# The last norm of a two-layer decoder trunk: its scales spread without a diagonal, one root for both sums, and one scaling moved behind the last sum

## The chip, the cores and the metric

The kernel runs on one core of a Trainium2 chip. The metric is the device time of one execution in microseconds (us). A core has a matrix engine (PE, with its weight loads listed apart as PEld), a vector engine (DVE), a scalar engine (ACT), GpSimd (POOL) and a queue engine (SP). Matrix products land in PSUM, which has eight banks of 512 f32 columns; POOL has no access to PSUM in this kernel. SP and ACT issue the transfers.

## What is computed

The reference runs two sub-layers over 1056 tokens (1024 of a prompt, 32 of a sample batch) of width 1024. The part that matters here is the end: the output projection of the second layer, the residual sum, and the final RMS norm.

```python
def _rmsnorm(x, gain):
    xf = x.astype(jnp.float32)
    y = xf * lax.rsqrt(jnp.mean(xf * xf, axis=-1, keepdims=True) + EPS)
    return (y * gain.astype(jnp.float32)).astype(x.dtype)

# _hgrn_layer ends with
    y = (o.reshape(Bsz, T, INNER_B) * jax.nn.silu(gate)).astype(x.dtype)
    return x + y @ w_out, S_T.astype(x.dtype)

# _trunk ends with
    return _rmsnorm(x, final_gain), jnp.stack(hs), jnp.stack(bufs), jnp.stack(Ss)
```

For each token, the squares of its 1024 values are summed, the root of their mean is inverted, and each value is multiplied by that scale and by its column's gain.

## The kernel before, in words

Activations are kept transposed: 8 tiles x2[k] of 128 features (partitions) by 1056 tokens (columns). In the profile these tiles carry the names of the buffers that they live in: k = 0 is ST, 1 to 3 are R, 4 is a, 5 to 7 are sg. A sum over features is thus a sum over partitions, which PE makes with a product with ones.

The last stage is the loop `for a, n in OUT` (L1762 on). It takes the tokens in three spans of n = 512, 288 and 256 columns. For each span it goes through the 8 tiles m = 0 to 7:

- PE makes the last three eighths of the output projection, 9 products of n columns (lines 262 to 264), into one of three banks.
- DVE adds that bank to x2[m] (L1781).
- ACT squares x2[m] (L1783).
- POOL adds the square to an accumulator `acc` (L1792). In the last span the squares of m = 4 to 7 aren't added by POOL; PE sums them straight into the column sums, behind all the products of the span.

The norm of a span is finished while the next span is worked on. At m = RM = 3 of the next span, `summed` has PE sum `acc` over partitions (`norm_sum`, L299), which puts the sum of token j of a group of 128 on partition j, one group to a column. `roots` then takes a root for each group on ACT (L1724), one reciprocal on DVE (L1727), and makes a diagonal on DVE (L1728, and L1732 for a rest of under 128): the identity times the reciprocal. At m = SM = 6, `spread` has PE multiply a matrix of ones by that diagonal (L1738), which puts the scale of token j on all partitions of column j of one bank. `finish` scales the 8 tiles with that bank and the gain. For the span of 512 all eight are done on DVE straight from PSUM (L1758). For the later spans tiles 5 to 7 go another way: ACT copies the bank to SBUF (L1751) and multiplies the tile by the gain (L1755), POOL multiplies by the copied scale (L1756). Each finished tile is written out by a transfer (L332), tiles of even k from SP, of odd k from ACT.

After the last span, PE runs two products of ones with ones (`spin`, L1796), and then the same roots, diagonal, spread and finish follow for the last 256 columns, now with nothing else running.

All of this is recorded into a `Flow` object, which plans the order of instructions on every engine from estimated costs (`add`, `plan`, `back`, `search`). Operations marked main=True on PE (the products, the `summed` sums and the spreads inside the loop) keep the order in which they are written. An engine carries out its instructions in the planned order, and waits at the first one that isn't ready. A transfer issued by ACT stands in ACT's own order, and ACT waits there until its tile is finished.

Two readers of one PSUM bank are kept apart: the second waits for a semaphore of the first.

Of the kernel before, what the change touches and what calls it, by code (L numbers as in the profile page):

```python
# [18 lines left out]
AF = mybir.ActivationFunctionType  # L19
ALU = mybir.AluOpType  # L20
# [11 lines left out]
SPOTS, SPOTS0, SPOTS1 = (-1, -1, 0, 2), (2, 5, -1, -1), (1, 5, 9, 13, 17, 20)  # L32
K2 = 8 - K1
NB4 = 6
RM, SM = 3, 6
OUT = ((0, 512), (512, 288), (800, 256))

D = 1024
# [192 lines left out]
def tile_trunk(ctx: ExitStack, tc: tile.TileContext, xT, prm, hc, w0, wg, wo0, w1, wo1, s_in,  # L231
# [18 lines left out]
    def pc(name, j, n=1):  # L250
        a = PRM[name][0] + j
        return P[:, a:a + n]
# [40 lines left out]
    def spans(n):  # L293
        return [(a, min(128, n - a)) for a in range(0, n, 128)]

    def norm_sum(sums, acc, n, start, stop):

        for s, (a, u) in zip(sums, spans(n)):
            T.matmul(s[:u], acc[:, a:a + u], ones[:, :1], start=start, stop=stop)  # L299

    def new_acts():
        hs, ls = [], []
# [15 lines left out]
    with ExitStack() as l0:  # L318
# [15 lines left out]
        def act(n, emit, r, w, prio=5, more=0.0):  # L334
            fl.add("ACT", 0.08 + 0.00086 * n + more, emit, r, w, prio)
# [5 lines left out]
        def pool(n, emit, r, w, prio=5):  # L341
            fl.add("POOL", 0.15 + 0.0022 * n, emit, r, w, prio)
# [609 lines left out]
    with ExitStack() as l1:  # L952
# [782 lines left out]
        def spread(n, dg, dk, main):  # L1735
# [2 lines left out]
            fl.add("PE", 0.002 * n, lambda: T.matmul(bc[:, :n], ones, dg, start=True, stop=True), (dk,), (bk,), 0, main=main)  # L1738
            return bc[:, :n], bk

        def summed(acc, ak, n):
            s, sk = next(hg)
            sums = [s[:, i:i + 1] for i in range(4)]
            fl.add("PE", 0.7, lambda: norm_sum(sums, acc, n, True, True), (ak,), (sk,), 0, main=True)
            return roots(n, sums, (sk,))

        def finish(a, n, bc, bk):
            q = slice(a, a + n)
            own = KD - 3 if a else KD
            if a:  # L1750
                act(n, lambda: S.copy(sb[0][:, :n], bc), (bk,), (sb[1],), 0)  # L1751
            for k in (*range(own, KD), *range(own)):
                x, xk = x2[k][:, q], ykeys(Y2 + k, a, n)
                if k >= own:
                    act(n, lambda x=x, k=k: S.activation(x, x, AF.Copy, scale=pc("gf", k)), xk, xk, 1)  # L1755
                    pool(n, lambda x=x: G.tensor_tensor(x, x, sb[0][:, :n], op=ALU.mult), (sb[1], *xk), xk, 1)  # L1756
                else:
                    dve(n, lambda x=x, k=k: V.scalar_tensor_tensor(x, x, pc("gf", k), bc, op0=ALU.mult, op1=ALU.mult), (bk, *xk), xk, 1)  # L1758
                dma(yT[k][:, q], x, xk, (), 1, n / 2, S if k % 2 else Q)

        for a, n in OUT:
            q = slice(a, a + n)  # L1762
            final = a + n == TOK
            cs = [c for c in range(NCH) if c * CH < a + n and (c + 1) * CH > a]
            acc, ak = next(accs)
            for m in range(KD):
                if a and m == RM:
                    dg = summed(*prev[:2], prev[3])
                if a and m == SM:
                    finish(*prev[2:], *spread(prev[3], *dg, True))  # L1770
                ps, pk = next(mm)
                hi, lo, wk = late[m]

                def emit(ps=ps, hi=hi, lo=lo, q=q, n=n):
                    for k in range(K2):
                        w = slice(128 * k, 128 * k + 128)
                        mm3(ps[:, :n], (hi[:, w], lo[:, w]), yh[K1 + k][:, q], yl[K1 + k][:, q], k == 0, k == K2 - 1)

                pe(9 * n / 2200, emit, (*wk, *((o, K1 + k, c) for o in ("xh", "xl") for k in range(K2) for c in cs)), (pk,))
                x, xk = x2[m][:, q], ykeys(Y2 + m, a, n)  # L1780
                dve(n, lambda x=x, ps=ps, n=n: V.tensor_tensor(x, ps[:, :n], x, op=ALU.add), (pk, *xk), xk, 0)  # L1781
                sq, sk = next(sqs) if m else (acc, ak)
                act(n, lambda sq=sq, x=x, n=n: S.activation(sq[:, :n], x, AF.Square), xk, (sk,), 1)  # L1783
                if final and m >= 4:
                    if m == 4:
                        sums = [(next(hg)) for _ in spans(n)]
                        sumk = [k for _, k in sums]
                        sums = [s[:, :1] for s, _ in sums]
                        fl.add("PE", 0.3, lambda acc=acc, n=n, sums=sums: norm_sum(sums, acc, n, True, False), (ak,), sumk, 0)
                    fl.add("PE", 0.3, lambda sq=sq, n=n, m=m, sums=sums: norm_sum(sums, sq, n, False, m == KD - 1), (sk, *sumk), sumk, 0)  # L1790
                elif m:
                    pool(n, lambda acc=acc, sq=sq, n=n: G.tensor_tensor(acc[:, :n], acc[:, :n], sq[:, :n], op=ALU.add), (sk, ak), (ak,), 1)  # L1792
            prev = acc, ak, a, n
        spin, wk = next(mm)
        for _ in range(2):
            fl.add("PE", 0.45, lambda: T.matmul(spin[:, :128], ones, ones, start=True, stop=True), sumk, (wk,), 0)  # L1796
        finish(a, n, *spread(n, *roots(n, sums, sumk), False))
        with tc.manual_schedule(engines={E.PE, E.DVE, E.Activation, E.Pool, E.SP}):
            fl.run(SEARCH, 60.0)

# [69 lines left out]
```

## Time and profile before

| | |
|---|---|
| median of 3 runs | 1032.07 us (1031.61 to 1032.12) |
| profiled execution | 1031.86 us |
| its span, first to last instruction | 1030.1 us, at a mean granted clock of 0.997 |
| PE busy | 1021.1 us (99%) |
| DVE, ACT, POOL busy | 810.8, 578.1, 496.5 us |
| last product of the output projection starts | 1019.11 us |
| last sum on PE starts | 1021.33 us |
| first scaling of the last span starts | 1024.08 us |
| last transfer is issued | 1026.43 us |

A row of the timeline reads: start (us from the span's start), duration (us), engine, line, operation, output <- inputs, shapes and types, number of merged instructions; in brackets the idle time of the engine before it and what ended it. A row of the windows table gives the stretch, its length, the busy time of PE, PEld, DVE, ACT and POOL with numbers of instructions, the granted PE clock, the share of the DMA engines and GB/s. On f32 operands each product written in the kernel shows as two weight loads and two matmuls.

### The profile page before, as it was taken

The page shows a single profiled execution, that of the slowest core. Times are in us where ns is not written, and L with a number is a line of the kernel's source. Part 1 is how long each engine was busy: PE and PEld are TensorE (multiplying, and loading weights), DVE is VectorE, ACT ScalarE, POOL GpSimd, SP SyncE. Part 2 cuts the span into 40 slices and gives each one's busy share as a digit, 9 for nine tenths or more (in the row PEclk, how much of TensorE's full clock was granted, in tenths as well). Part 3 has the DMA queues.
Part 4 walks back from the last instruction along what each step waited for, and adds up shares of the span by engine and source line. Part 5 has one row for each costly group of instructions (what it writes and reads, how often), then busy time and mean ns, then how long its engine had stood idle before and what let it go on. Part 6 is the DMA issues. An engine that isn't in the chain of part 4 may idle for free.

```text
span 1030.1 us, 26451 instructions
## 1 busy us (share of the span) xinstructions
PE 1021.1 (99%) x10118; PEld 996.4 (97%) x10118; DVE 810.8 (79%) x1641; ACT 578.1 (56%) x1322; POOL 496.5 (48%) x569
## 2 busy tenths in 40 slices
PE   9999999999999999999999999999999999999997
PEld 9999999999999999999999999999999999999986
DVE  7999785867888699436599999798989799986436
ACT  8788747876775785335454463626363636552334
POOL 0117353544526236636425656555555557533544
PEclk9999999999999999999999999999999999999998
DMA  9201112112852487426474244343535353687204
GB/s 299 78 17 56 57 48 74 52 54 76 257 178 59 133 270 223 160 83 219 136 213 138 73 147 132 130 148 111 167 111 168 102 159 122 207 246 209 87 1 169
DMA packets 107854, 138.30 MB, mean 134 GB/s; under 512 B 23632, under 2 KB 85072, under 8 KB 107728
## 3 DMA queue, kind: packets, MB, share of 16 engines
q1 hardware_dynamic: 105424, 133.85, 42.1%
q10 hardware_dynamic: 2304, 2.77, 0.8%
q8 instruction: 79, 1.29, 0.5%
q14 instruction: 47, 0.39, 0.1%
HBM read 89.99 MB, written 41.61 MB: 128 GB/s over the span
## 4 chain that ended last, share of the span: by engine, by line
PE 93%; DVE 2%; DMA 2%; ACT 1%; issue 1%; POOL 1%; SPq 0%; POOLq 0%; DVEq 0%; ACTq 0%
PE mm L262 27%; PE mm L264 26%; PE mm L263 26%; PE hg L1085 2%; PE hg L592 1%; PE hg L262 1%; PE hg L264 1%; PE hg L263 1%; PE hg L753 1%; PE hg L1232 1%; PE hg L1287 1%; PE hg L1289 1%; DMA k<-yd 1%; PE mm L1085 0%; DMA vt<-sg 0%
## 5 line engine op out<-in xcount | busy, mean ns | idle before, releaser
L262 PE MATMUL mm<-xh,whi 128*128 128x352 f32 (+1 forms) x1127 | 352.6, 313 | 0.1
L264 PE MATMUL mm<-xh,wlo 128*128 128x352 f32 (+1 forms) x1127 | 348.1, 309 | 0.0
L263 PE MATMUL mm<-xl,whi 128*128 128x352 f32 (+1 forms) x1127 | 347.7, 309 | 0.0
L346 POOL TENSOR_TENSOR wlo<-wraw,whi 128x256 fp32r<-128x256 f32 (+3 forms) x188 | 200.8, 1084 | 199.7 <-ACT whi L403 97.3
L263 PEld LDWEIGHTS mm<-xl,whi 128*128 128x128 f32 x1127 | 212.5, 189 | 1.4 <-DVE xl L346 0.3
L262 PEld LDWEIGHTS mm<-xh,whi 128*128 128x128 f32 x1127 | 211.8, 188 | 2.1 <-DVE k L1545 0.3
L264 PEld LDWEIGHTS mm<-xh,wlo 128*128 128x128 f32 x1127 | 212.0, 188 | 0.0
L524 DVE SCALAR_TENSOR_TENSOR k<-xb,prm_sb,k 128x352 f32<-128x352 f32 (+2 forms) x144 | 82.3, 596 | 24.2 <-ACT k L521 20.7
L262 PE MATMUL mm<-t,whi 128*128 128x264 f32 (+1 forms) x330 | 96.6, 293 | 0.2 <-issue 0.2
L264 PE MATMUL mm<-t,wlo 128*128 128x264 f32 (+1 forms) x330 | 94.4, 286 | 0.0
L263 PE MATMUL mm<-t,whi 128*128 128x264 f32 (+1 forms) x330 | 94.4, 286 | 0.0
L1545 DVE TENSOR_TENSOR k<-mm,k 128x264 f32<-128x264 f32 x154 | 64.0, 424 | 11.7 <-PE mm L264 10.3
L346 POOL TENSOR_TENSOR wlo<-R,whi 128x256 fp32r<-128x256 f32 x70 | 58.3, 854 | 27.0 <-ACT whi L1469 24.1
L607 POOL TENSOR_TENSOR k<-X 128x352 f32<-128x352 f32 x36 | 43.6, 1217 | 52.8 <-DVE R L608 42.0
L1469 ACT CAST whi<-wraw 128x512 fp32r<-128x512 f32 x56 | 34.5, 618 | 60.4 <-DVE wraw L1479 26.0
L403 ACT CAST whi<-wraw 128x512 fp32r<-128x512 f32 (+2 forms) x79 | 44.3, 572 | 39.1 <-PE mm L263 28.9
L262 PEld LDWEIGHTS mm<-t,whi 128*128 128x128 f32 x330 | 62.1, 188 | 1.5 <-issue 0.3
L263 PEld LDWEIGHTS mm<-t,whi 128*128 128x128 f32 x330 | 62.2, 188 | 0.0
L264 PEld LDWEIGHTS mm<-t,wlo 128*128 128x128 f32 x330 | 62.1, 188 | 0.0
L262 PE MATMUL mm<-yh,whi 128*128 128x352 f32 x153 | 52.2, 341 | 0.0
L264 PE MATMUL mm<-yh,wlo 128*128 128x352 f32 x153 | 49.4, 323 | 0.0
L263 PE MATMUL mm<-yl,whi 128*128 128x352 f32 x153 | 49.4, 323 | 0.0
(458 smaller groups left out, 2513.9 us busy)
## 6 DMA issues: line engine op xcount, KB each, us to landing
wraw<-in_w_dram SPq DMA_DIRECT2D x88, 256.0 KB, 3.0
wraw<-in_wo_dram SPq DMA_DIRECT2D x34, 192.0 KB, 2.5
R<-in_w_dram SPq DMA_DIRECT2D x17, 256.0 KB, 3.9
si<-in_s_in_dram SPq DMA_DIRECT2D x8, 512.0 KB, 5.4
vt<-sg SPq DMA_DIRECT2D x8, 512.0 KB, 3.8
sg<-vt SPq DMA_DIRECT2D x32, 128.0 KB, 2.9
kt<-kt SPq DMA_DIRECT2D x8, 512.0 KB, 3.6
kt<-kt SPq DMA_DIRECT2D x32, 128.0 KB, 5.1
```

What stands on the lines that cost most here:

```text
L262: T.matmul(out, wh, xh, start=first, stop=False)
L263: T.matmul(out, wh, xl, start=False, stop=False)
L264: T.matmul(out, wl, xh, start=False, stop=last)
L346: emit = lambda: e.tensor_tensor(b, x, a.bitcast(F32), op=ALU.subtract)
L403: act(m, lambda hi=hi, raw=raw, m=m: S.copy(hi[:, :m], raw[:, :m]), rk, (hk,), prio)
L524: dve(u, lambda src=src, dst=dst, sh=sh, k=k: V.scalar_tensor_tensor(dst, sh(src, k), pc("cw", 12 * k + m), dst, op0=ALU.mult, op1=ALU.add ...
L592: fl.add("PE", 0.62, lambda ps=ps, i=i, c=c: T.matmul(ps[:96, :CH], gs[:, i, :], ST[:96, chunk(c)], start=True, stop=True), (("gs",), *((" ...
L607: pool(CH, lambda x=x, a=a, b=b: G.tensor_tensor(x, a.bitcast(F32), b.bitcast(F32), op=ALU.add), (ak, bk), (xk,), 3)
L753: fl.add("PE", 0.25, lambda: T.matmul(warm[:, :128], ones, ones, start=True, stop=True), (), (wk,), 9)
L1085: T.matmul(ps[32 * j:32 * j + 32, n * w:n * w + w], B[:, o:o + 32], q(slice(o, o + 32)), start=True, stop=True, tile_position=(0, 32 * j))
L1469: act(512, lambda: S.copy(hi, raw), (rk,), (hk,), 2)
L1545: dve(QT, lambda: V.tensor_tensor(o[0], z[0], u[0], op=ALU.add), (z[1], u[1]), (o[1],), 0)
```

## The change

Four edits, all in the last stage.

- The spread of the **last** span no longer takes a diagonal. `spread_last` takes the column of reciprocals r of a group of 128 as the stationary operand, repeated over 128 columns with a step of zero, and the identity as the moving one; the product holds r[j] in column j on all partitions. It is called twice, into two banks: ACT copies the first, DVE scales from the second.
- `last_sum` puts both sums of the last span into two columns of one bank, so that one root (L1822 of the new file) takes both; only the first product clears the bank.
- SM goes from 6 to 5: the spread of the preceding span stands ahead of tile 5 of the running span, and not ahead of tile 6. This holds for the span of 512 (finished within the span of 288) and for the span of 288 (finished within the span of 256).
- When the span of 288 is finished, tiles 4 to 7 go by ACT and POOL (before: 5 to 7), tiles 0 to 2 are scaled on DVE at once, and tile 3 is scaled on DVE only after the last sum of x2[7] (L1805 of the new file), by `rest`.

```diff
-RM, SM = 3, 6
+RM, SM = 3, 5
...
+    def last_sum(s, acc, n, first, last):
+
+        for i, (a, u) in enumerate(spans(n)):
+            T.matmul(s[:u, i:i + 1], acc[:, a:a + u], ones[:, :1], start=first and not i, stop=last, skip_group_check=True)
...
+        def spread_last(n, r, rk):
+
+            bc, bk = next(hg)
+
+            def emit():
+                for i, (a, u) in enumerate(spans(n)):
+                    T.matmul(bc[:, a:a + u], r[:, i:i + 1].to_broadcast([128, 128]), ident, start=True, stop=True)
+
+            fl.add("PE", 0.0018 * n, emit, (rk,), (bk,), 0)
+            return bc[:, :n], bk
...
-        def finish(a, n, bc, bk):
+        def scaled(k, q, a, n, bc, bk, after=()):
+
+            x, xk = x2[k][:, q], ykeys(Y2 + k, a, n)
+            dve(n, lambda: V.scalar_tensor_tensor(x, x, pc("gf", k), bc, op0=ALU.mult, op1=ALU.mult), (bk, *xk, *after), xk, 1)
+            dma(yT[k][:, q], x, xk, (), 1, n / 2, S if k % 2 else Q)
+
+        def finish(a, n, bc, bk, copied, ck, now):
             q = slice(a, a + n)
-            own = KD - 3 if a else KD
+            own = KD - (3 if a + n == TOK else 4) if a else KD
             if a:
-                act(n, lambda: S.copy(sb[0][:, :n], bc), (bk,), (sb[1],), 0)
-            for k in (*range(own, KD), *range(own)):
+                act(n, lambda: S.copy(sb[0][:, :n], copied), (ck,), (sb[1],), 0)
+            for k in (*range(own, KD), *range(min(now, own))):
+                if k < own:
+                    scaled(k, q, a, n, bc, bk)
+                    continue
                 x, xk = x2[k][:, q], ykeys(Y2 + k, a, n)
...
+            return lambda after: [scaled(k, q, a, n, bc, bk, after) for k in range(now, own)]
...
                 if a and m == SM:
-                    finish(*prev[2:], *spread(prev[3], *dg, True))
+                    got = spread(prev[3], *dg, True)
+                    rest = finish(*prev[2:], *got, *got, 3 if final else KD)
...
-        finish(a, n, *spread(n, *roots(n, sums, sumk), False))
+        rest(ykeys(Y2 + KD - 1, a, n))
+        w = n // 128
+        r, rk = next(nr2)
+        act(4, lambda: S.activation(r[:, :w], sums[:, :w], AF.Sqrt, bias=epsc, scale=1.0 / D), (sumk,), (rk,), 0)
+        dve(16, lambda: V.reciprocal(r[:, :w], r[:, :w]), (rk,), (rk,), 0)
+        copied = spread_last(n, r, rk)
+        finish(a, n, *spread_last(n, r, rk), *copied, KD)
```

The planner made a new order from this. On all engines it differs from the old one only from the span of 288 on. Three places follow, each first before, then after.

On PE, in the span of 288: `hg_165<-sg_153,ones_80` is the spread of the span of 512, products into `mm_162` are tile 4, into `mm_163` tile 5, into `mm_160` tile 6. Before:

```order
L264 MATMUL mm_162<-t41_5211,xl_104 128x288
L262 MATMUL mm_163<-t30_5208,xl_106 128x288
L263 MATMUL mm_163<-t30_5208,xl_106 128x288
L264 MATMUL mm_163<-t30_5208,xl_106 128x288
L262 MATMUL mm_163<-t40_5210,xl_106 128x288
L263 MATMUL mm_163<-t40_5210,xl_106 128x288
L264 MATMUL mm_163<-t40_5210,xl_106 128x288
L262 MATMUL mm_163<-t41_5211,xl_106 128x288
L263 MATMUL mm_163<-t41_5211,xl_106 128x288
L264 MATMUL mm_163<-t41_5211,xl_106 128x288
L1738 MATMUL hg_165<-sg_153,ones_80 128x512
L262 MATMUL mm_160<-t30_5208,xl_108 128x288
```

After:

```order
L263 MATMUL mm_162<-t41_5211,xl_104 128x288
L264 MATMUL mm_162<-t41_5211,xl_104 128x288
L1743 MATMUL hg_165<-sg_153,ones_80 128x512
L262 MATMUL mm_163<-t30_5208,xl_106 128x288
L263 MATMUL mm_163<-t30_5208,xl_106 128x288
L264 MATMUL mm_163<-t30_5208,xl_106 128x288
```

The spread stands nine products earlier. In the span of 256 the spread of the span of 288 has moved in the same way.

On DVE, at the end of the span of 256: L1781 (before) and L1805 (after) are the residual sums of 256 columns (`sg_150`, `sg_148`, `sg_152` are tiles 5, 6 and 7), L1758 and L1766 the scalings, L1728 the diagonal. Before:

```order
L1781 TENSOR_TENSOR sg_150<-mm_162,sg_150 128x256
L1758 SCALAR_TENSOR_TENSOR ST_147<-ST_147,prm_sb_74,mm_161 128x288
L1758 SCALAR_TENSOR_TENSOR R_73<-R_73,prm_sb_74,mm_161 128x288 x2
L1781 TENSOR_TENSOR sg_148<-mm_163,sg_148 128x256
L1758 SCALAR_TENSOR_TENSOR R_73<-R_73,prm_sb_74,mm_161 128x288
L1758 SCALAR_TENSOR_TENSOR a_114<-a_114,prm_sb_74,mm_161 128x288
L1781 TENSOR_TENSOR sg_152<-mm_160,sg_152 128x256
L1727 RECIPROCAL nr20_5230<-nr20_5230 128x2
L1728 TENSOR_TENSOR sg_153<-ident_75,nr20_5230 128x256
L1758 SCALAR_TENSOR_TENSOR ST_147<-ST_147,prm_sb_74,hg_165 128x256
```

After:

```order
L1766 SCALAR_TENSOR_TENSOR R_73<-R_73,prm_sb_74,hg_164 128x288
L1766 SCALAR_TENSOR_TENSOR ST_147<-ST_147,prm_sb_74,hg_164 128x288
L1766 SCALAR_TENSOR_TENSOR R_73<-R_73,prm_sb_74,hg_164 128x288
L1805 TENSOR_TENSOR sg_150<-mm_162,sg_150 128x256
L1805 TENSOR_TENSOR sg_148<-mm_163,sg_148 128x256
L1805 TENSOR_TENSOR sg_152<-mm_160,sg_152 128x256
L1766 SCALAR_TENSOR_TENSOR R_73<-R_73,prm_sb_74,hg_164 128x288
L1823 RECIPROCAL nr20_5230<-nr20_5230 128x2
L1766 SCALAR_TENSOR_TENSOR ST_147<-ST_147,prm_sb_74,hg_165 128x256
```

The three scalings stand ahead of the sums of tiles 5 to 7, one stands behind them, the scaling of `a_114` and the diagonal are gone.

On ACT, at the same place: L1783 and L1807 are the squares, L1755 and L1779 the products with the gain, DMA rows are issues of finished tiles. Before:

```order
L1783 ACTIVATE a_115<-sg_148 128x256
L1755 ACTIVATE sg_148<-sg_148,prm_sb_74 128x256
L332 DMA out_yT_dram<-R_73 128x288
L1783 ACTIVATE sg_153<-sg_152 128x256
L1755 ACTIVATE sg_152<-sg_152,prm_sb_74 128x256
L332 DMA out_yT_dram<-sg_152 128x288
L1724 ACTIVATE nr20_5230<-hg_167,eps_85 128x1
L1724 ACTIVATE nr20_5230<-hg_164,eps_85 128x1
L1751 COPY sg_149<-hg_165 128x256
```

After:

```order
L1807 ACTIVATE a_115<-sg_148 128x256
L1779 ACTIVATE sg_148<-sg_148,prm_sb_74 128x256
L337 DMA out_yT_dram<-sg_152 128x288
L1807 ACTIVATE sg_153<-sg_152 128x256
L1779 ACTIVATE sg_152<-sg_152,prm_sb_74 128x256
L337 DMA out_yT_dram<-R_73 128x288
L1822 ACTIVATE nr20_5230<-hg_167,eps_85 128x2
L1773 COPY sg_149<-mm_161 128x256
```

The issue of tile 7 of the span of 288 (`sg_152`), which POOL finishes, stands ahead of the last square; the issue of tile 3 (`R_73`), which DVE finishes, has taken its old place. On POOL a product for `a_114` is put ahead of the three of the span of 288.

More of the change, by code (lines that the diff above doesn't have):

```diff
@@ L1745, in summed @@
             return roots(n, sums, (sk,))
-        def finish(a, n, bc, bk):
+        def scaled(k, q, a, n, bc, bk, after=()):
[3 more added lines that the diff above has]
+        def finish(a, n, bc, bk, copied, ck, now):
             q = slice(a, a + n)
-            own = KD - 3 if a else KD
+            own = KD - (3 if a + n == TOK else 4) if a else KD
             if a:
-                act(n, lambda: S.copy(sb[0][:, :n], bc), (bk,), (sb[1],), 0)
-            for k in (*range(own, KD), *range(own)):
-                x, xk = x2[k][:, q], ykeys(Y2 + k, a, n)
[L1754 to L1758, printed above, removed]
+                act(n, lambda: S.copy(sb[0][:, :n], copied), (ck,), (sb[1],), 0)
[3 more added lines that the diff above has]
+                    continue
+                x, xk = x2[k][:, q], ykeys(Y2 + k, a, n)
+                act(n, lambda x=x, k=k: S.activation(x, x, AF.Copy, scale=pc("gf", k)), xk, xk, 1)
+                pool(n, lambda x=x: G.tensor_tensor(x, x, sb[0][:, :n], op=ALU.mult), (sb[1], *xk), xk, 1)
                 dma(yT[k][:, q], x, xk, (), 1, n / 2, S if k % 2 else Q)
+            return lambda after: [scaled(k, q, a, n, bc, bk, after) for k in range(now, own)]
         for a, n in OUT:
@@ L1785, in tile_trunk @@
                     if m == 4:
[L1786 to L1790, printed above, removed]
+                        sums, sumk = next(hg)
+                        fl.add("PE", 0.45, lambda acc=acc, n=n, sums=sums: last_sum(sums, acc, n, True, False), (ak,), (sumk,), 0)
+                    fl.add("PE", 0.45, lambda sq=sq, n=n, m=m, sums=sums: last_sum(sums, sq, n, False, m == KD - 1), (sk, sumk), (sumk,), 0)
                 elif m:
@@ L1795, in tile_trunk @@
         for _ in range(2):
-            fl.add("PE", 0.45, lambda: T.matmul(spin[:, :128], ones, ones, start=True, stop=True), sumk, (wk,), 0)
-        finish(a, n, *spread(n, *roots(n, sums, sumk), False))
+            fl.add("PE", 0.45, lambda: T.matmul(spin[:, :128], ones, ones, start=True, stop=True), (sumk,), (wk,), 0)
+        rest(ykeys(Y2 + KD - 1, a, n))
[5 more added lines that the diff above has]
+        finish(a, n, *spread_last(n, r, rk), *copied, KD)
         with tc.manual_schedule(engines={E.PE, E.DVE, E.Activation, E.Pool, E.SP}):
```

## The prediction

> **What bounds the kernel now.** I read the page's first and fourth parts, then the timeline of the last 30 us engine by engine, then windows of the end.
>
> ```profile
> PE 1021.1 (99%) x10118; PEld 996.4 (97%) x10118; DVE 810.8 (79%) x1641; ACT 578.1 (56%) x1322; POOL 496.5 (48%) x569
> PE 93%; DVE 2%; DMA 2%; ACT 1%; issue 1%; POOL 1%; SPq 0%; POOLq 0%; DVEq 0%; ACTq 0%
> ```
>
> PE is the bound up to its last product. So there are two questions: does the change make PE's stream longer, and does it make shorter what follows. First the place where PE waits in the span of 288.
>
> ```profile
> 1004.56 0.29 PE L264 MATMUL mm<-t,xl 128*128 128x288 f32 x1
> 1004.69 0.30 PE L262 MATMUL mm<-t,xl 128*128 128x288 f32 x1
> ...
> 1005.75 0.29 PE L264 MATMUL mm<-t,xl 128*128 128x288 f32 x1
> 1006.25 1.12 PE L1738 MATMUL hg<-sg,ones 128*128 128x512 f32 x2 [0.22 <-DVE sg L1728]
> 1002.63 1.28 ACT L1724 ACT_TABLE_LOAD   x1
> 1004.60 0.40 ACT L1724 ACTIVATE nr<-mm,eps 128x1 f32<-128x1 f32 x2
> 1005.27 0.17 DVE L1727 RECIPROCAL nr<-nr 128x4 f32<-128x4 f32 x1
> 1005.47 0.73 DVE L1728 TENSOR_TENSOR sg<-ident,nr 128x512 f32<-128x512 f32 x1
> ```
>
> Tile 5 runs from 1004.69 to 1005.75, and then the spread has to wait until 1006.25: the diagonal ends at 1005.47 + 0.73 = 1006.20. PE is already there too early.
>
> Then the end, after PE's last product.
>
> ```profile
> 1019.11 0.28 PE L264 MATMUL mm<-t,xl 128*128 128x256 f32 x1
> 1019.23 0.50 PE L299 MATMUL hg<-ones,R 128*128 128x1 f32 x4
> 1020.04 1.03 PE L299 MATMUL hg<-ones,a 128*128 128x1 f32 x8
> 1021.33 0.61 PE L299 MATMUL hg<-ones,sg 128*128 128x1 f32 x4 [0.26 <-ACT sg L1783]
> 1021.79 0.69 PE L1796 MATMUL mm<-ones 128*128 128x128 f32 x4
> 1022.94 0.70 PE L1738 MATMUL hg<-sg,ones 128*128 128x256 f32 x2 [0.46 <-DVE sg L1728]
> 1020.34 0.42 DVE L1781 TENSOR_TENSOR sg<-mm,sg 128x256 f32<-128x256 f32 x1
> 1022.26 0.17 DVE L1727 RECIPROCAL nr<-nr 128x2 f32<-128x2 f32 x1 [1.50 <-ACT nr L1724]
> 1024.08 0.48 DVE L1758 SCALAR_TENSOR_TENSOR ST<-ST,prm_sb,hg 128x256 f32<-128x256 f32 x1 [1.20 <-ACT sg L1751]
> 1020.86 0.42 ACT L1783 ACTIVATE sg<-sg 128x256 f32<-128x256 f32 x1 [0.18 <-DVE sg L1781]
> 1021.37 0.34 ACTq L332 DMA_DIRECT2D out_yT_dram<-sg  x1
> 1021.75 0.48 ACT L1724 ACTIVATE nr<-hg,eps 128x1 f32<-128x1 f32 x2
> 1023.68 0.37 ACT L1751 COPY sg<-hg 128x256 f32<-128x256 f32 x1 [1.45 <-PE hg L1738]
> 1024.13 2.09 POOL L1756 TENSOR_TENSOR sg<-sg 128x256 f32<-128x256 f32 x3 [3.45 <-ACT sg L1751]
> 1026.43 0.42 ACTq L332 DMA_DIRECT2D out_yT_dram<-sg  x1
> ```
>
> The last product ends at 1019.11 + 0.28 = 1019.39, but its residual sum starts only at 1020.34: DVE was behind by 0.95. From there it is a pure chain: sum 1020.34, square 1020.86, column sum 1021.33, roots 1021.75, reciprocal 1022.26, diagonal, spread 1022.94, copy 1023.68, scalings 1024.08 and 1024.13. The execution took 1031.86 us, 1.76 more than its span and 0.21 under the median of the runs, 1032.07. I take the changes in us against this profile and add the sum to the median.
>
> **The change part by part.** *The spread of 512 stands nine products earlier (+1.19).* On ACT, DVE and PE nothing is reordered ahead of this diagonal, so it still ends at 1006.20 and the spread still starts at 1006.25. What ran in the shadow of that wait was tile 5: 9 products at a pitch of 0.13, from 1004.69 to 1005.88. Now PE comes to the spread at 1004.69, sits for about 1.56 instead of 0.37, and does tile 5 afterwards. All that follows on PE is later by 1.19. This has no cover: PE carries out its main products in the order written. DVE gains air behind it, and that is worth nothing to PE.
>
> *The spread of 288 stands nine products earlier (+0.12).*
>
> ```profile
> 1015.46 0.28 PE L264 MATMUL mm<-t,xl 128*128 128x256 f32 x1
> 1016.65 0.65 PE L1738 MATMUL mm<-sg,ones 128*128 128x288 f32 x2
> 1014.56 0.18 DVE L1727 RECIPROCAL nr<-nr 128x3 f32<-128x3 f32 x1
> 1015.47 0.23 DVE L1732 TENSOR_SCALAR sg<-ident,nr 128x32 f32<-128x32 f32 x1
> 1017.33 0.51 DVE L1758 SCALAR_TENSOR_TENSOR ST<-ST,prm_sb,mm 128x288 f32<-128x288 f32 x1
> 1017.88 0.40 ACT L1751 COPY sg<-mm 128x288 f32<-128x288 f32 x1
> 1018.36 0.81 POOL L1756 TENSOR_TENSOR sg<-sg 128x288 f32<-128x288 f32 x1 [1.83 <-ACT sg L1751]
> 1018.36 2.32 POOL L1756 TENSOR_TENSOR sg<-sg 128x288 f32<-128x288 f32 x3 [1.83 <-ACT sg L1751]
> ```
>
> PE would come to it after the product at 1015.46, at 1015.58 on the old clock, 1016.77 on the new. The diagonal was whole at 1015.47 + 0.23 = 1015.70. In the new order a residual sum still stands between its two parts; DVE is 0.1 less behind. My estimate from the durations of these rows (root of the rest at 1015.38 on the new clock, reciprocal 1015.64, diagonal 1015.84, sum 1016.26, rest 1016.60) gives 1016.83, and PE starts at about 1016.88. So +0.12; bounds 0 (ready in time) and +0.4 (reciprocal no earlier than before relative to PE, and a restart after the wait). PE's last product is later by 1.31 in all.
>
> *The last residual sum no longer waits for DVE (-0.38, not -0.95).* With three scalings ahead and one behind, DVE is idle when the last product ends. But PE has 16 passes of column sums queued ahead of the last one. Eight of them start at 1020.04 at a pitch of 0.11 (the row of eight lasts 1.03, its last pass some 0.27), so the last four could start at 1020.95 at the earliest, against 1021.33. The gain is 0.38; the rest of the 0.95 is lost in PE's queue. On the new clock: 1020.95 + 1.31 = 1022.26.
>
> *An issue on ACT that waits for POOL now stands ahead of the last square (+0.35).* The copy of the 288 bank follows DVE's first scaling: spread at 1016.88, scaling 0.68 later, copy 0.55 later, POOL 0.48 later, at 1018.59. POOL has four products there, not three, at 2.32/3 = 0.77: they end at 1021.68. Only then can ACT issue tile 7, for 0.34, and the last square, behind it, starts at about 1022.1, though its tile was ready at 1021.25. It takes 0.42, and the last sum starts at 1022.6, not 1022.26. Bounds: 0 (POOL at 0.70 each, as in its row of 256 columns, the issue then ahead of need) and +0.5 (POOL at the 0.81 of its first product). The scaling left behind the last sum costs nothing: it starts at about 1021.2 and takes 0.51, the reciprocal isn't due before 1023.5, and the issue that waits for it on ACT has 1 us until the root.
>
> *One root for two (0).* The two roots take 0.48, but the first runs while PE makes the second sum: the four passes end at 1021.33 + 0.61 = 1021.94, and the roots at 1022.23, one root (0.26) behind that. The single root has to wait for the same pass. Bounds -0.05 and +0.05.
>
> *No diagonal (-0.45).* From reciprocal to spread it was 1022.94 - 1022.26 = 0.68. Without it: the reciprocal's 0.17 and a hop of 0.06 (as between diagonal and spread), 0.23.
>
> *Two spreads into two banks (+0.03).* Before, from the spread's start, DVE began 1.14 later and POOL 1.19 later, since ACT's copy (0.37) came first on the same bank. Now each bank takes four passes of 128 columns; the nearest row is the spin, four in 0.69 at a pitch of 0.11. ACT begins 0.73 after the start as before, POOL too at 1.19. DVE's bank is full at 0.69 + 0.44 = 1.13, DVE begins at 1.17. So DVE no longer waits for the copy, but for PE, and just as long. Stationary operands with a step of zero are in no row; I take the usual load, and +0.2 as the upper bound. [...]
>
> *The tail (0).*
>
> ```profile
> 1025.00:1025.50 0.50, 0.00 (x0) 0.00 (x0) 0.50 (x2) 0.00 (x0) 0.50 (x2) 0.50 0.10 37
> 1025.50:1026.00 0.50, 0.00 (x0) 0.00 (x0) 0.50 (x2) 0.00 (x0) 0.50 (x2) 0.50 0.93 316
> 1028.00:1028.50 0.50, 0.00 (x0) 0.00 (x0) 0.00 (x0) 0.00 (x0) 0.00 (x0) 0.50 1.05 348
> ```
>
> The eight tiles (1.05 MB) flow out without a gap from 1025.5 to 1028.5 at about 340 GB/s. That takes 3.1 us from the first tile on, whoever is last. ACT now issues POOL's tile first and its last issue comes perhaps 0.15 sooner; the flow hides that. Bounds -0.15 and +0.2.
>
> **The sum.** +1.19 + 0.12 - 0.38 + 0.35 - 0.45 + 0.03 = +0.86. The profile's 1031.86 becomes 1032.72, the median 1032.07 becomes 1032.9. A measurement of this kernel can tell about 0.2% from no change, 2.06 us, so this is no change.
>
> **The rivals.**
>
> *The issue doesn't hold ACT up.* POOL's product or ACT's copy comes a little sooner, and the term of +0.35 falls away: 1032.6. For it: the slack is only some tenths. Against: four products at 0.77 are longer than the time there is.
>
> *The first wait doesn't lengthen PE's stream.* If the diagonal came by 1004.7, the change would be 0.86 - 1.19 = -0.33: 1031.7. Against: the table load (1.28) and the roots behind it end at 1005.00 and stand where they stood. Even so it isn't faster by 2 us: without both waits and without ACT's hold-up it is -0.8, 1031.3.
>
> *The clock falls while PE waits (slower).* The granted clock of the end:
>
> ```profile
> 1023.00:1023.50 0.50, 0.50 (x2) 0.24 (x2) 0.00 (x0) 0.00 (x0) 0.00 (x0) 1.00 0.00 0
> ...
> 1024.00:1024.50 0.50, 0.00 (x0) 0.00 (x0) 0.42 (x2) 0.05 (x1) 0.37 (x1) 0.50 0.00 0
> ```
>
> It went to 0.50 within 0.5 us of PE's last pass, after a stretch with waits of only 0.26 and 0.46 but many passes of one column. A wait of 1.56 is longer than any in these rows. If the clock halves there, each tile of 288 columns takes 1.19 more; one to three tiles until it comes back: +1.2 to +3.5, with 2.0 as a middle 1032.9 + 2.0 = 1034.9. It decides over the sign that can be measured from one tile on. Against: the wait stands amid dense products. [...]
>
> *The clock falls before the last spreads.* The same fall at 1023.7 on an unmoved clock would meet the spreads, which now run from about 1023.8 to 1024.9. At half pace eight passes take 0.88 more: DVE starts 0.88 later, POOL 0.44. That gives 1033.3 to 1033.8, say 1033.6.
>
> **How the numbers follow.** The forecast 0.57, ACT not held 0.15, the late fall of the clock 0.12, the first wait hidden 0.08, the fall at the wait 0.08. The bounds of the terms, taken all at once, carry the forecast from 1032.2 to 1033.8, and runs of one kernel scatter by 0.25 on either side: 1031.8 to 1034.0 holds these and leaves out the fall at the wait and part of the hidden wait. Faster by over 2.06 us follows from none of the cases, 0.02 for what I don't see; slower the fall at the wait, 0.07; the rest 0.91.
>
> **What would show it.** Right: in the span of 288 the spread still starts near 1006.25 after an idle time of over 1.4; the last product starts near 1020.4; the last residual sum follows it without DVE waiting; the last square waits behind an issue for POOL; reciprocal to spread 0.23; DVE's first scaling waits for PE, near 1024.9. Wrong: a spread that starts before 1006, a granted clock under 1.00 between 1006 and 1020, a square that starts right after its residual sum, or an end that moves without its first tile moving.

## The result, and the profile after

The changed kernel takes 1033.55 us (median of 16 runs, 1032.31 to 1035.96) against 1032.01 us of the kernel before (16 runs beside it). The ratio is 1.0017, its 95% interval 1.001 to 1.0023. The ratio is under the 0.2% which the prediction set as its bound, so the change counts as no difference; but the whole interval lies above 1, and its upper end passes that bound. The profiled execution took 1034.04 us, with a span of 1032.2.

The page of the kernel after, parts 1 and 4, reads almost as before:

```profile
PE 1021.8 (99%) x10124; PEld 996.5 (97%) x10124; DVE 810.2 (78%) x1638; ACT 578.6 (56%) x1322; POOL 500.3 (48%) x570
PE 90%; DVE 3%; DMA 3%; ACT 1%; issue 1%; POOL 1%; SPq 0%; ACTq 0%; DVEq 0%; POOLq 0%
```

PE's share of the chain fell from 93 to 90%, DVE's and DMA's rose. The place is found in the timeline of the last 31 us, first PE, then DVE, ACT and POOL. Its first row is the column sum of the span of 512. It started at 1001.41 before, so the two executions stand 0.47 apart when they enter the code that was changed, and from here on I measure from that start.

```profile
1001.88 0.95 PE L299 MATMUL mm<-ones,R 128*128 128x1 f32 x8
...
1006.70 1.12 PE L1743 MATMUL hg<-sg,ones 128*128 128x512 f32 x2 [1.38 <-DVE sg L1733]
...
1017.55 0.75 PE L1743 MATMUL hg<-sg,ones 128*128 128x288 f32 x2 [0.17 <-DVE sg L1737]
...
1021.21 0.28 PE L264 MATMUL mm<-t,xl 128*128 128x256 f32 x1
...
1022.14 1.03 PE L304 MATMUL hg<-ones,a 128*128 128x1 f32 x8
1023.41 0.60 PE L304 MATMUL hg<-ones,sg 128*128 128x1 f32 x4 [0.24 <-ACT sg L1807]
1023.88 0.69 PE L1818 MATMUL mm<-ones 128*128 128x128 f32 x4
1024.57 0.88 PE L1752 MATMUL mm<-ident,nr 128*128 128x128 f32 x4
1025.24 1.06 PE L1752 MATMUL hg<-ident,nr 128*128 128x128 f32 x4
1016.24 0.77 DVE L1733 TENSOR_TENSOR sg<-ident,nr 128x256 f32<-128x256 f32 x1
1021.53 0.42 DVE L1805 TENSOR_TENSOR sg<-mm,sg 128x256 f32<-128x256 f32 x1 [0.60 <-PE mm L264]
1024.35 0.17 DVE L1823 RECIPROCAL nr<-nr 128x2 f32<-128x2 f32 x1 [1.97 <-ACT nr L1822]
1026.34 0.48 DVE L1766 SCALAR_TENSOR_TENSOR ST<-ST,prm_sb,hg 128x256 f32<-128x256 f32 x1 [1.83 <-PE hg L1752]
1022.50 0.34 ACTq L337 DMA_DIRECT2D out_yT_dram<-sg  x1
1022.94 0.42 ACT L1807 ACTIVATE sg<-sg 128x256 f32<-128x256 f32 x1 [0.39 <-issue]
1024.05 0.26 ACT L1822 ACTIVATE nr<-hg,eps 128x2 f32<-128x2 f32 x1 [0.16 <-PE hg L304]
1028.49 0.39 ACTq L337 DMA_DIRECT2D out_yT_dram<-sg  x1
1016.00 0.73 POOL L1814 TENSOR_TENSOR R<-R,a 128x256 f32<-128x256 f32 x1 [0.28 <-ACT nr L1729]
1020.13 2.33 POOL L1780 TENSOR_TENSOR sg<-sg 128x288 f32<-128x288 f32 x3
```

PE waits twice, at 1006.70 for the diagonal of the span of 512 and at 1017.55 for that of the span of 288. The last residual sum (DVE, 1021.53) follows its product at once. The last square (ACT, 1022.94) stands behind an issue (1022.50) that waited for POOL, whose products end at 1020.13 + 2.33 = 1022.46. And the second spread takes 1.06 for four passes, where the spin before it took 0.69. The windows of the end say why:

```profile
1024.00:1024.50 0.50, 0.50 (x5) 0.37 (x4) 0.15 (x1) 0.26 (x1) 0.00 (x0) 1.00 0.37 122
1024.50:1025.00 0.50, 0.50 (x4) 0.44 (x4) 0.01 (x1) 0.00 (x0) 0.00 (x0) 0.97 0.54 173
1025.00:1025.50 0.50, 0.50 (x5) 0.50 (x4) 0.00 (x0) 0.02 (x1) 0.00 (x0) 0.50 0.00 0
```

The granted clock (third number from the end) falls to half near 1024.97, in the middle of the spreads.

Here are the steps of every run in us behind the start of the column sum of 512, read from the timelines. "Stretch" is the last one, the start of ACT's last issue.

```
                spread  last     last   reciprocal  last    first DVE  stretch
                of 512  product  sum                spread  scaling
before           4.84   17.70    19.92   20.85      21.53    22.67     25.02
after            4.82   19.33    21.53   22.47      22.69    24.46     26.61
e1_sm6           4.84   17.71    19.69   20.92      21.14    23.23     25.38
e2_sm5           4.82   19.39    21.43   22.37      23.05    24.71     27.30
e3_spread        4.84   17.71    19.93   20.86      21.30    23.25     25.40
e4_wide          4.82   19.35    21.57   22.61      22.83    24.03     26.24
e5_table         3.28   17.70    19.91   20.84      21.07    22.26     24.46
e6_best          4.47   17.23    19.13   20.10      20.32    21.51     23.92
e8_onebank       4.81   19.34    21.55   22.59      22.81    23.96     26.31
e9_sp7           4.82   19.30    21.20   22.15      22.37    23.57     26.02
```

Before to after the stretch grew by 1.59 us. With the 0.47 from earlier stages and some 0.1 around the end that makes the 2.18 between the two profiled executions; the medians differ by 1.54. Each stretch is read from one execution, and the 16 times of one kernel spread over 3.6 us and more, so that the two differences agree this well is partly chance.

### The profile page after: what moved, and what is told of

It is laid out like the page before. It is cut to its first block, busy times and chain, and to the rows that moved or that the text cites. A ratio compares the mean times of both kernels' runs of the same rounds, so it can differ in the third digit from the quotient of the medians.

```text
span 1032.2 us, 26459 instructions
## 1 busy us (share of the span) xinstructions
PE 1021.8 (99%) x10124; PEld 996.5 (97%) x10124; DVE 810.2 (78%) x1638; ACT 578.6 (56%) x1322; POOL 500.3 (48%) x570
## 4 chain that ended last, share of the span: by engine, by line
PE 90%; DVE 3%; DMA 3%; ACT 1%; issue 1%; POOL 1%; SPq 0%; ACTq 0%; DVEq 0%; POOLq 0%
PE mm L262 26%; PE mm L263 25%; PE mm L264 25%; PE hg L1090 2%; PE hg L597 1%; PE hg L262 1%; PE hg L264 1%; PE hg L263 1%; PE hg L1237 1%; PE hg L1292 1%; PE hg L1294 1%; DVE t L351 1%; DMA sg<-xn 1%; DMA sg<-in_xT_dram 1%; DMA wraw<-in_w_dram 1%
```

## The experiments

My theory after the result: the early spreads cost 1.19 and 0.44, the ends of the chain gain and lose as forecast, and a fall of the clock at the last spreads adds 0.6. Rivals: the column operand with a step of zero makes each pass slow, and not the clock; the second bank costs; ACT is late for something other than POOL.

**e1_sm6: the spreads back in their old place.** Two parts of the change taken apart: here all is kept but the place.

```
-RM, SM = 3, 5
+RM, SM = 3, 6
```

> The changed kernel with SM back at 6: only the move of the two spreads is undone. I measure E, from the start of the column sum of the span of 512 on PE (in the span of 288) to the start of the last issue on ACT: 25.02 us before (1001.41 to 1026.43), 26.61 after (1001.88 to 1028.49). Theory (the moved spreads cost 1.19 for tile 5 and 0.44 at the second wait): PE's last product comes 17.7 behind the column sum as before, not 19.33; the last sum on PE comes 0.38 sooner than before; E = 24.5 if the clock holds until the spreads are done, 25.1 if it falls; 0.5 to 0 us faster than before. Rival (the loss sits in the four products on POOL and the scaling put behind the last sum): E stays above 26.

The ratio to the kernel before is 0.9996 (0.9984 to 1.0007). The last product is back at 17.71, so both waits come from the place alone. The last sum comes 0.23 sooner than before, where 0.38 was forecast for a residual sum that DVE does not delay. The rows at the end:

```profile
1018.81 0.51 ACT L1779 ACTIVATE sg<-sg,prm_sb 128x256 f32<-128x256 f32 x1
...
1019.31 0.42 ACT L1807 ACTIVATE sg<-sg 128x256 f32<-128x256 f32 x1
1019.82 0.34 ACTq L337 DMA_DIRECT2D out_yT_dram<-R  x1
1020.25 0.41 ACTq L337 DMA_DIRECT2D out_yT_dram<-sg  x1
1020.71 0.26 ACT L1822 ACTIVATE nr<-hg,eps 128x2 f32<-128x2 f32 x1 [0.45 <-PE hg L304]
1017.80 2.31 POOL L1780 TENSOR_TENSOR sg<-sg 128x288 f32<-128x288 f32 x3
1021.23 1.20 PE L1752 MATMUL mm<-ident,nr 128*128 128x128 f32 x4 [0.29 <-DVE nr L1823]
```

The last square (1019.31) starts when ACT's own product with the gain ahead of it (1018.81 + 0.51) ends, which is why 0.15 of the 0.38 are missing. The issue of tile 7 (1020.25) has moved on: it now stands ahead of the root instead of the last square, behind the issue of tile 3 (1019.82, taking 0.34), and the root follows the last sum (1019.78) by 0.93, where it was 0.64 in the kernel after. Here it is not a wait for POOL, whose fourth product ends at 1017.80 + 2.31 = 1020.11, before the issue of tile 3 does; the two issues in a row hold the root up. The clock falls at 1021.29, in the first pass of the spread. So the gain of the parts at the end is eaten by these two, and the stretch is 0.36 longer than before.

**e2_sm5: the early spreads alone, put into the kernel before.**

```
-RM, SM = 3, 6
+RM, SM = 3, 5
```

> The kernel before with SM 5 and nothing else. Theory: PE idle 1.4 to 1.5 ahead of the first spread and some 0.3 ahead of the second, last product 19.3 behind the column sum; the last residual sum no longer late, which is worth 0.38; E = 25.02 + 1.63 - 0.38 = 26.3, 1.2 us slower than before. Rival (the moved spreads are hidden, the loss comes with the new end): E at 25.0, no change.

Ratio 1.001 (1.0001 to 1.0019), the stretch 27.30, a us more than expected. The last product is 1.69 later than before, where the prediction had 1.31 for the two early spreads, and here is most of the error of its second term, without any of the other edits:

```profile
1005.79 1.12 PE L1738 MATMUL hg<-sg,ones 128*128 128x512 f32 x2 [1.38 <-DVE sg L1728]
1016.75 0.72 PE L1738 MATMUL mm<-sg,ones 128*128 128x288 f32 x2 [0.21 <-DVE sg L1732]
1015.34 0.79 DVE L1728 TENSOR_TENSOR sg<-ident,nr 128x256 f32<-128x256 f32 x1
1015.10 0.74 POOL L1792 TENSOR_TENSOR R<-R,a 128x256 f32<-128x256 f32 x1 [0.29 <-ACT nr L1724]
```

The diagonal takes 0.79 where it took 0.49 before, with a POOL operation (L1792) beside it. The extra us lies further on, since the expected 26.3 held 1.63 for the last product already. The last sum is 0.26 later than expected (it follows the last product by 2.04, not by 2.22 - 0.38). The clock falls near 1023.17, ahead of the spread, and from spread to DVE's first scaling it takes 1.66 instead of 1.14. From there to the last issue it takes 2.59 instead of 2.35.

**e3_spread: only the end without a diagonal, with two banks and one root.** SM at 6, POOL at three tiles, nothing put behind the last sum:

```
-RM, SM = 3, 5
+RM, SM = 3, 6
-            own = KD - (3 if a + n == TOK else 4) if a else KD
+            own = KD - 3 if a else KD
-                    rest = finish(*prev[2:], *got, *got, 3 if final else KD)
+                    rest = finish(*prev[2:], *got, *got, KD)
```

> The kernel before with the new end of the last span alone (one bank for the sums, one root, no diagonal, two spreads), SM 6, tiles 5 to 7 on POOL, nothing put behind the last sum. Theory: reciprocal to spread 0.22 in place of 0.68; DVE begins 1.17 behind the spread if the clock holds, up to 1.8 if it falls. E = 24.6 or 25.2. Rival (a stationary operand with a step of zero is slow by itself): passes of 0.21 at a granted clock of 1.00, E = 25.2 whatever the clock.

Ratio 0.9987 (0.9978 to 0.9997): over its 11 runs this kernel is a little faster than the kernel before, though its profiled execution, in which the clock fell early, has a stretch 0.38 longer. Up to the reciprocal the table shows the kernel before to 0.01: the one root is worth nothing, as forecast. From the reciprocal to the spread it takes 0.44 instead of 0.68, not 0.23, since the spin ahead of the spread is at half clock already (four passes in 1.11, against 0.69), and the passes of the spread too. The windows show three steps of the clock:

```profile
1022.50:1023.00 0.50, 0.50 (x5) 0.50 (x6) 0.00 (x0) 0.35 (x2) 0.00 (x0) 0.89 1.02 339
...
1026.00:1026.50 0.50, 0.00 (x0) 0.00 (x0) 0.50 (x3) 0.00 (x0) 0.50 (x1) 0.70 0.00 0
...
1029.50:1030.00 0.50, 0.00 (x0) 0.00 (x0) 0.00 (x0) 0.00 (x0) 0.00 (x0) 0.72 0.90 297
```

A mean of 0.89 over half a us is full clock for 0.39 and half for 0.11, a fall at 1022.89; in the same way the clock rises at 1026.30 and falls at 1029.72. The steps are 3.41 and 3.42 apart. Idle time alone doesn't tell where it falls: in the kernel after the clock stays at 1.00 through the wait of 1.38 that ends at 1006.70 and up to 1024.50, and here PE isn't idle ahead of the fall. From 1020.22 on it made 20 passes of one column, with a wait of 0.26 ahead of the last four, and the first pass of the spin.

**e4_wide: the last sums 128 columns wide.** If the passes of one column are what lets the clock fall, wider ones should hold it. The sums are multiplied by 128 equal columns, which puts the same number into each, and the root reads one of them:

```
-            T.matmul(s[:u, i:i + 1], acc[:, a:a + u], ones[:, :1], ...)
+            T.matmul(s[:u, a:a + 128], acc[:, a:a + u], ones, ...)
```

> The changed kernel with the last column sums made 128 columns wide (128 equal columns for each sum, the root reads the first of each), so that PE moves more in the same number of passes. Theory (the clock fell at 1024.97 since the sums move one column a pass): the sums keep their pitch of 0.11, the granted clock stays at 1.00 until the spreads are done, passes of 0.11 in both spreads, DVE begins 1.17 behind the spread and not 1.77, E = 26.0. Rival (the stationary operand with a step of zero is slow by itself): second bank still 0.21 a pass at a clock of 1.00, E = 26.6. If the sums become longer, they add 0.1 to 0.5.

Ratio 1.0001 (0.999 to 1.0012). The timeline of PE and DVE, and one window behind the spreads:

```profile
1020.89 1.06 PE L304 MATMUL hg<-ones,a 128*128 128x128 f32 x8
...
1022.64 0.61 PE L1818 MATMUL mm<-ones 128*128 128x128 f32 x4
1023.36 0.71 PE L1752 MATMUL mm<-ident,nr 128*128 128x128 f32 x4
1023.91 0.61 PE L1752 MATMUL hg<-ident,nr 128*128 128x128 f32 x4
1024.56 0.48 DVE L1766 SCALAR_TENSOR_TENSOR ST<-ST,prm_sb,hg 128x256 f32<-128x256 f32 x1 [1.25 <-PE hg L1752]
```

```profile
1024.00:1024.50 0.50, 0.50 (x5) 0.33 (x3) 0.00 (x0) 0.37 (x1) 0.00 (x0) 1.00 0.00 0
```

Eight wide passes take 1.06 against 1.03. Behind the last sum the reciprocal comes 1.04 later, against 0.94, and that is the largest part of what the stretch (26.24) is over the expected 26.0. The clock stays at 1.00 (up to 1026.50), the second spread starts 0.55 behind the first (0.67 in the kernel after), and DVE starts 1.20 behind the spread instead of 1.77. Four passes of the second spread take 0.61, as the four of the spin do. So in this run the column operand with a step of zero costs nothing over the spin's, and the clock is what made the spreads slow in the kernel after. In the whole time the gain is not clear: the interval of the ratio overlaps that of the kernel after.

One profile is no proof of the sums as the cause: e5_table below keeps its clock at 1.00 through both spreads with narrow sums. The mean clock of every timed run helps. At 0.997 half the clock is missing for (1 - 0.997) x 2 x 1030 = 6.2 us, about from the last spreads to the end of the span. This is a rough mark: e3's profiled run has 0.998 though its clock fell ahead of the spreads, because it rose again behind them. With narrow sums 45 of 62 runs are at 0.997 or under (after 12 of 16, e1 8 of 12, e2 12 of 12, e3 5 of 11, e5 8 of 11); with wide sums 1 of 44 (e4, e6, e8 none, e9 1 of 10). Only after and e4 differ in the sums alone: 12 of 16 against none of 12. The times go the same way: the runs above 0.997 have a mean of 1033.1 us in after, 1031.3 in e1, 1031.8 in e3 and 1031.4 in e5, the others of 1033.8, 1033.2, 1032.3 and 1032.5.

The sums are not the whole of it. The kernel before was run beside e1 to e9 too, and all 73 of those runs at its usual time are at 0.997 or under, as are the 12 of e2; both have the old spread of two passes of 256 columns. The new end, with its eight passes of 128 columns, keeps narrow sums above 0.997 in 17 of 50 runs.

**e5_table: the table of the root loaded early.** The diagonal of 512 ends late because ACT loads a table for 1.28 us ahead of the roots. A root of a constant pulls that load into the span of 512:

```
-                act(n, lambda sq=sq, x=x, n=n: S.activation(sq[:, :n], x, AF.Square), xk, (sk,), 1)
+                act(n, lambda sq=sq, x=x, n=n: S.activation(sq[:, :n], x, AF.Square), xk if a or m < 6 else (*xk, "pre"), (sk,), 1)
+                if not a and m == 5:
+                    act(4, lambda: S.activation(pre, epsc, AF.Sqrt), (sk,), ("pre",), 0)
```

The squares of tiles 6 and 7 of that span now wait for this root, which keeps it in its place in ACT's order.

> The changed kernel with the table for the square root loaded early: a root of a constant stands on ACT behind the square of tile 5 in the span of 512, so that the four roots of this span need no load behind its column sum. Theory (the first wait comes from the table load of 1.28 us in front of the roots): the diagonal is ready about 1.2 us sooner, PE waits 0.2 us or less at the spread of 512 instead of 1.38, and from the column sum of 512 to the last issue it takes 26.61 - 1.2 = 25.4 us (24.8 if the clock also holds at the last spreads), so about 1032.3 where the changed kernel is at 1033.5. Rival (something else holds the diagonal, DVE's queue for instance): the spread still starts about 4.8 us behind the column sum and the stretch stays at 26.6 us.

```profile
995.38 1.28 ACT L1810 ACT_TABLE_LOAD   x1
...
1002.64 0.70 ACT L1730 ACTIVATE nr<-mm,eps 128x1 f32<-128x1 f32 x4
1004.82 1.02 PE L1744 MATMUL hg<-sg,ones 128*128 128x512 f32 x2
```

The spread of 512 starts 3.28 behind the column sum, with no wait, and the last product is back at 17.70 in spite of SM = 5. So this early spread costs only because its scales are not ready. The second wait is still there (the diagonal of 288 takes 0.79 here too, and the spread waits 0.33 for its scales); e6 below, without either wait, has its last product at 17.23. The stretch is 24.46, lower than the 24.8 expected with a clock that holds (in this profile it is at 1.00 up to 1027.00); the ratio is 0.9996 (0.9987 to 1.0005).

**e6_best: what paid, without what cost.** SM at 6, three tiles for POOL, tiles 3 and 4 of the span of 288 scaled behind the last sum, wide sums, the early table load, and the end of the change:

```
-            own = KD - (3 if a + n == TOK else 4) if a else KD
+            own = KD - 3 if a else KD
```

with the edits of e1, e4 and e5.

> The parts of the change that paid, without those that cost: SM back at 6, POOL back at three tiles of the span of 288, tiles 3 and 4 of it on DVE behind the last sum, no diagonal and two banks as in the change, sums of the last span 128 columns wide, and the early table load. Theory (each part is worth what the runs before showed): 25.02 of the kernel before, -0.37 for its first wait, -0.38 for the last residual sum, -0.45 for the diagonal, +0.1 for what is left, gives 23.9 us from the column sum of 512 to the last issue, about 1 us under the kernel before, 1031.0. Rival (the gain is given back at the end, the clock falls in spite of the wide sums, or an issue still holds ACT): 24.5 us or more, the same as the kernel before within 0.5 us.

The stretch is 23.92, 1.10 under the kernel before, as expected to 0.02. The median is 1030.75 against 1032.65 of the kernel before beside it; the ratio is 0.9983 (0.9974 to 0.9992). This version is faster than the kernel before, by an amount at the edge of what can be told. It was not run beside the changed one, whose ratio to the kernel before lies above 1.

**e7_pool3: three tiles for POOL, the rest of the change kept.**

> The changed kernel with POOL at three tiles of the span of 288 instead of four (tiles 3 and 4 are scaled on DVE behind the last sum). Theory (ACT's issue of tile 7 waits for POOL's fourth product and holds the last square up): the last square starts right behind its residual sum, the last sum about 0.36 us sooner, 26.61 - 0.36 = 26.25 us from the column sum of 512 to the last issue if the clock falls as in the changed kernel. Rival (something else holds the last square, or DVE's second scaling behind the last sum delays the reciprocal by as much): 26.6 us or more.

The edit is the one line shown under e6. This run answers nothing. With this edit the planner put DVE and ACT in another order from the middle of the program on, the column sum of 512 starts at 1008.26 and not at 1001.88, and part of the first output came out wrong, from a cause that stays open. Its ratio of 1.0063 (1.005 to 1.0075) is that of another program, and nothing is read from it. e9_sp7 asks the same question in another way.

**e8_onebank: wide sums, and one bank for the last spread.**

```
-        finish(a, n, *spread_last(n, r, rk), *copied, KD)
+        finish(a, n, *copied, *copied, KD)
```

> The changed kernel with the wide sums of the earlier run, and one spread bank at the end instead of two: ACT copies it, then DVE scales from it. Theory (the second bank buys nothing, since DVE waits for its passes as long as for the copy): at full clock DVE's first scaling starts 1.15 us behind the spread's start, against 1.20 with two banks, POOL's first product at 1.2 in both, and the stretch from the column sum of 512 to the last issue stays at 26.2 us. Rival (two readers of one bank cost more than the copy's 0.37 us): DVE starts 1.5 us or more behind the spread, and the stretch is 0.3 us longer.

```profile
1025.39 0.71 PE L1752 MATMUL mm<-ident,nr 128*128 128x128 f32 x4
1026.14 0.37 ACT L1773 COPY sg<-mm 128x256 f32<-128x256 f32 x1 [1.00 <-PE mm L1752]
1026.54 0.48 DVE L1766 SCALAR_TENSOR_TENSOR ST<-ST,prm_sb,mm 128x256 f32<-128x256 f32 x1 [1.21 <-ACT sg L1773]
```

DVE starts 1.15 behind the spread, against 1.20 with two banks. The wait for the copy and the wait for the second bank's passes are worth the same; the second bank buys nothing. The stretch is 26.31 against 26.24, the ratio 1.0008 (0.9999 to 1.0017).

**e9_sp7: wide sums, and tile 7 of the span of 288 issued by SP.**

```
-                dma(yT[k][:, q], x, xk, (), 1, n / 2, S if k % 2 else Q)
+                dma(yT[k][:, q], x, xk, (), 1, n / 2, S if k % 2 and (k < KD - 1 or a + n == TOK) else Q)
```

> The changed kernel with wide last sums, and the transfer of tile 7 of the span of 288 issued by SP instead of ACT, so that ACT does not wait for POOL there; POOL keeps its four products. Theory (that issue holds the last square up): the last square starts 0.1 us behind its residual sum's end or sooner after the square's predecessor on ACT, the last sum about 0.36 us sooner against the last product than with the issue on ACT, and 26.24 - 0.36 = 25.9 us from the column sum of 512 to the last issue. Rival (ACT is late for another reason): 26.2 us or more.

```profile
1021.35 0.42 ACT L1807 ACTIVATE a<-sg 128x256 f32<-128x256 f32 x1
1021.80 0.51 ACT L1779 ACTIVATE sg<-sg,prm_sb 128x256 f32<-128x256 f32 x1
1022.27 0.42 ACT L1807 ACTIVATE sg<-sg 128x256 f32<-128x256 f32 x1
```

No issue stands ahead of the last square, and the last sum starts 21.20 behind the column sum instead of 21.57 in e4. Of these 0.37, 0.05 is a last product that is sooner (the planner also put a residual sum ahead of the diagonal of 288 here, which then takes 0.42 behind POOL's addition); 0.32 is the price of ACT's wait. The first scaling is 0.46 sooner, but only 0.22 of it reaches the last issue; the issues of tiles 1 and 3 run later against POOL's last product here. A difference of this size does not show in the whole time (ratio 1.0009, 0.9997 to 1.0022).

**e10_pool2: POOL kept free while DVE makes the diagonal of 288.** PE sums the squares of tiles 2 and 3 too:

```
-                if final and m >= 4:
-                    if m == 4:
+                if final and m >= 2:
+                    if m == 2:
```

> The changed kernel with wide last sums, where POOL adds only the square of tile 1 in the span of 256 and PE sums tiles 2 and 3 as well, so that POOL does nothing while DVE makes the diagonal of the span of 288. Theory (the diagonal takes 0.77 to 0.79 us because POOL's product runs beside it): it takes 0.42 to 0.45 us, and is ready about 0.35 us sooner behind its reciprocal. Rival (the product has nothing to do with it): 0.77 us again. The end is not compared, since PE has four more passes of sums ahead of the spread and eight more at the end.

```profile
1015.53 0.18 DVE L1732 RECIPROCAL nr<-nr 128x3 f32<-128x3 f32 x1 [0.69 <-ACT nr L1729]
1015.74 0.42 DVE L1733 TENSOR_TENSOR sg<-ident,nr 128x256 f32<-128x256 f32 x1
1014.49 0.74 POOL L1814 TENSOR_TENSOR R<-R,sg 128x256 f32<-128x256 f32 x1 [1.10 <-ACT sg L1807]
```

POOL is done at 1015.23, and the diagonal takes 0.42. Both parts of it (the rest of 32 columns included) are ready 1.12 behind the reciprocal's start, against 1.47 in the kernel after. This is one execution, of 1033.75 us. In the kernel before, POOL's addition covered the first part of it only:

```profile
1014.71 0.42 DVE L1781 TENSOR_TENSOR R<-mm,R 128x256 f32<-128x256 f32 x1
1015.05 0.49 DVE L1728 TENSOR_TENSOR sg<-ident,nr 128x256 f32<-128x256 f32 x1
1014.53 0.73 POOL L1792 TENSOR_TENSOR R<-R,a 128x256 f32<-128x256 f32 x1 [0.27 <-ACT nr L1724]
```

There POOL ends at 1015.26 and the diagonal at 1015.54, 0.28 later. In the kernel after POOL ends at 1016.73 and the diagonal at 1017.01, again 0.28 later; in e2_sm5 at 1015.84 and 1016.13, 0.29. So the diagonal isn't slowed in proportion: in all three POOL is still at work when it starts, and it ends 0.28 to 0.29 after POOL. The theory holds, in a sharper form than it was stated. The diagonal has both inputs in SBUF; the residual sum at 1014.71 in the kernel before, which has one in PSUM, took 0.42 with POOL at work from its start to its end. Why the one takes longer beside POOL and the other doesn't, no run here shows.

## Why the prediction was right, and where it was not

The verdict and the time hold: 1033.55 lies in the range, 0.65 above the 1032.9, and on the side of the bound that was given 0.91. That the median fell inside is partly luck. Two terms were too small by 0.92 together, and the range was drawn with a scatter of 0.25 on either side, taken from three runs; the 16 runs of the kernel after lie from 1.24 under to 2.41 above their median. Term by term, in the stretch:

- **Spread of 512, +1.19:** the last product of the preceding tile, the wait (1.38 idle, just under the 1.4 given as its sign) and the spread's start came as worked out; the column sum of 288 behind it is 1.17 later (1012.77 before, 1014.41 after, less the 0.47). e1 and e2 show that the place does it, e5 that the table load is what the spread waits for. The rival that hides this wait did not happen by itself, but e5 makes it happen.
- **Spread of 288, +0.12:** mis-sized, it was 0.44 (1.63 for both waits to the last product), just over the upper bound of 0.4. The step that failed is the diagonal's duration "from the durations of these rows". On the new clock POOL starts its addition 0.24 ahead of the diagonal, which takes 0.77 and ends 0.28 behind POOL; e10 measures 0.42 with POOL idle. By this the spread starts 0.20 later than forecast (1017.55 less the 0.47, against 1016.88); the other 0.12 lie behind its start, where the spread takes 0.75 after its wait and 0.65 in the kernel before and in e10, without one.
- **Last residual sum -0.38 and ACT's issue +0.35:** together the last sum is 1.61 later while the last product is 1.63 later, -0.02. e9 measures 0.32 for the issue. e1 adds that it doesn't vanish by a change of place: it stands ahead of the root there, and takes its 0.41 though POOL is done.
- **One root, 0:** from sum to reciprocal 0.93 before, 0.94 after.
- **No diagonal, -0.45:** 0.68 became 0.22, -0.46.
- **Two banks, +0.03:** at full clock 1.20 instead of 1.14 (e4), +0.06, and one bank does as well (e8). In the profiled run it was 1.77, +0.63: this is the rival "the clock falls before the last spreads", which I gave 0.12. It forecast 1033.3 to 1033.8, and the measured median lies there. The mistake was the chance. I took the instant of the fall from one execution, 22.29 behind the column sum of 512; in the others where it comes by the end of the spreads it lies 20.50 (e3), 21.20 (e1), 22.20 (e2) and 23.09 (after) behind it, and 12 of the 16 runs have a mean clock of 0.997 or under. Part of the agreement with that rival's time comes from the second wait, which it did not hold.
- **The tail, 0:** from the first scaling to the last issue 2.35 became 2.15, -0.20, just outside its lower bound of -0.15; the flow behind it ends 3.7 later in both.

The sum: 0.86 + 0.32 (second wait) + 0.60 (clock) - 0.20 (tail) + 0.01 = 1.59, the measured stretch. The other slow rival, a fall of the clock at the wait of 1.4, did not happen: the clock is at 1.00 from there to 1024.9. Its one to three tiles at half clock were an estimate with no run behind it.

What stays open is how little work makes the clock fall, and when. With narrow sums most runs have a mean clock of 0.997 or under, with wide ones almost none, but no run here varied the number of columns between 1 and 128, and none changed the spin. The profiles give no one delay either. In the kernel before the clock falls 0.06 behind the end of PE's last pass (1023.70 against 1023.64). In e6 a mean of 0.77 from 1025.00 to 1025.50 puts the fall at 1025.27, 4.03 behind that end (1021.24). In e5 the clock is still at 1.00 at 1027.00, 3.24 behind it (1023.76), and in after, e1, e2 and e3 it falls ahead of the last pass.

## What to carry to other kernels

Before a consumer is moved forward on an engine that never rests, look up when its input is ready: what ran in the shadow of the old wait is what the move costs, and a table load ahead of that input may be moved instead (in e5 the spread came 1.54 us sooner that way, with one tiny instruction). An issue that waits for a slow engine holds what stands behind it on its own queue (the last square by 0.32 here, by e9), and even without a wait it takes its time there (0.34 and 0.41 in e1), so a new place for it only chooses what is held. And a long tail of tiny matmuls may cost more than its own time: with sums of one column 12 of 16 runs had a mean clock of 0.997 or under (after), with the same sums made 128 columns wide none of 12 (e4), for 0.03 us more in eight passes and 0.10 more from the last of them to the reciprocal.

## What the runs showed of the hardware

- A 128x256 multiplication on DVE with both inputs in SBUF took 0.42 alone (e10_pool2), and with a POOL addition running at its start it ended 0.28 to 0.29 after that addition, whether it had started 0.21 or 0.50 ahead of POOL's end (before, after, e2_sm5).
- The granted clock fell though PE had not been idle for more than 0.24 us since its last product (after, to 0.50 near 1024.97), behind passes of one column, the spin and three or four passes of the spread; and it stayed at 1.00 through a wait of 1.38 us between dense products (after, up to 1006.70).
- With a stationary operand with a step of zero (one column repeated over 128) four passes of the second spread took 0.61, as the four of the spin did with a plain one (e4).
